# Decode pages in two rings, keys and values apart, with one rounding buffer fewer and the gates' cache laid out heads first

## The chip, the cores and the metric

The kernel runs on one core of one Trainium2 chip. The metric is the time of one execution on the device in microseconds (us); what is compared is the median of several executions. A trace of one execution, taken by the hardware profiler, gives the times of single instructions.

## The reference: what is computed

One step of a hybrid decoder layer, in 32-bit floating point, for two groups of rows that share the weights: a prompt of 1024 tokens, and eight samples with one new token each. Every row is normed and multiplied by `w_in`; the columns are the queries, keys, values and forget logits of 8 attention heads and the two inputs of 8 gating heads. The two groups of heads are normed, joined and multiplied by `w_o`. A cross attention with 4 heads into 256 memory tokens follows (`w_cq`, `w_co`), then a gated feed-forward network (ffn) with a causal convolution of width 3 (`w_up`, `w_down`, inner width 2816), and a final norm.

Each sample attends to its own past of 8192 tokens, which lies in 64 pages of 128 tokens:

```python
k_all = jnp.concatenate([k_pool[page_table].reshape(B, past, H, hd), k.astype(k_pool.dtype)], axis=1)
v_all = jnp.concatenate([v_pool[page_table].reshape(B, past, H, hd), v.astype(v_pool.dtype)], axis=1)
lf_all = jnp.concatenate([logf_pool[page_table].reshape(B, past, H).astype(jnp.float32), logf], axis=1)
c = jnp.cumsum(lf_all, axis=1)
```

The scores get the difference of the running sums `c` of the forget logits (the gates) before the softmax. Per sample that is 16 MB of keys and 16 MB of values, read once.

## The kernel before

The prompt and the samples are two streams of work. The prompt comes in stages: projections (`p1`), attention of two groups of rows, then for each half of 512 rows the output product of `w_o` (`mid`), the cross attention with its own output product (`out_proj` with `w_co`, L1063 to L1083), and the ffn. A large product on TensorE (PE) is made of three passes (L272 to L274, or L280, L281 and L284 where only half the rows are ready): a weight tile `wr` comes from memory (four buffers), ScalarE (ACT) rounds it into `wh` (L235, `WH` = 5 buffers), VectorE (DVE) makes the rest `wl` (L236, four buffers). Rows are normed and split in the same way: after the cross attention, DVE adds the product to the row (L1015), the row is scaled by its norm's factor (ACT, or DVE in L1045), PE turns it (L1124), and ACT and DVE split it (L238, L239) for the first products of `w_up`.

The samples' stream is `decode()`: for each sample 16 key steps and, a sample and two steps later (`VLAG`), 16 value steps in pairs. A key step (`kstep`) gathers a page of 1 MB (128 partitions x 2048 numbers) by an indirect DMA of GpSimd (POOL, L1428); DVE multiplies it by the query (L1444, in place) and sums over a head (L1448), in two pieces each in some stages. A value step (`vstep`) gathers its page (L1489), and PE multiplies it by the softmax's weights into one accumulator `dv` (L1495). All pages lie in one pool of `NKV` = 4 buffers, `kv`, and so do the weights and memory pages that the samples use later (L1568) and the prompt's rows at the start (L401). A page can be fetched when the one that had its buffer has been used. POOL issues the gathers in order; an issue whose buffer is not free holds up the ones behind it.

The gates of a sample are loaded at its 12th key step (L1404), brought from the order (token, head) into (head, token) by a copy on ACT (L1407), and scanned on DVE (L1408). They, the query tiles, the masks of `dv` and small tiles of the later stage share a pool of five 512-wide buffers, `d2`. The softmax of a sample is eight small steps on DVE (from L1460 on) with ACT and PE between.

The two streams are woven together by a table of paces: after so many units of the prompt's work, one step of the samples' stream is written. The framework then sets each engine's order with a model of times of its own, so buffers and priorities, not the code's order alone, decide what stands where. When the last sample is done, `sample_rest` takes the samples through `w_o`, the cross attention, and the ffn beside the prompt's second ffn.

## Time and profile before

| what | value |
| --- | --- |
| runs shown | 1798.83, 1797.29, 1791.11 us; median 1797.29 |
| profiled execution | 1793.69 us, span of its instructions 1791.7 us |
| mean granted clock of TensorE | 0.993 |
| moved by DMA | 521.06 MB, 291 GB/s in the mean |
| POOL's queue of gathers and pages | 341.14 MB, 50.0% of the DMA engines' time |
| SP's queue of weights | 165.73 MB, 26.5% |

PE is the engine with the most work. Its instructions run in the order written, and one that waits holds up all behind it; the same is true of the other engines. An idle gap in front of an instruction is put down to what released it, so the reader can ask at each gap whose work came last. The prediction uses three kinds of answers of the trace: the busy time of each engine in stretches of the span, the waits (engine, line, what it waited for, total, times, longest), and single instructions in order of time (start, duration, engine, line).

### The profile page before, as it was taken

To read this page: it belongs to the slowest core of one execution; us is meant where nothing else is said; L and a number is where in the kernel's file an instruction comes from. 1 tells how busy PE (TensorE), PEld (TensorE's weight loads), DVE (VectorE), ACT (ScalarE), POOL (GpSimd) and SP (SyncE) were. 2 spreads that over 40 slices of the span, in tenths; PEclk is the share of its full clock that TensorE was granted. 3 is DMA by queue.
4 is the path that set the end of the run, shared out by engine and by line. 5 is a ranking of instruction groups with operands and counts; after the bars stand their busy time and mean duration, and the time that the engine had idled before them with its cause. 6 is when DMAs were issued, how large, how long until landed. Compare 5 with 4: busy or idle time off the path is not lost.

```text
span 1791.7 us, 25124 instructions
## 1 busy us (share of the span) xinstructions
PE 1735.9 (97%) x9653; PEld 1285.7 (72%) x9653; DVE 1399.9 (78%) x1733; ACT 733.5 (41%) x1374; POOL 488.3 (27%) x461
## 2 busy tenths in 40 slices
PE   8999999889999999999999999999999999999997
PEld 5787777655677666767777777766666778768875
DVE  4689658989788986989999999898885549855344
ACT  6332355566643635333333244335353233333232
POOL 1252234443222332333322223433322112102110
PEclk9999999999999999999999999999999999999999
DMA  8786798777697975779788788988879587568982
GB/s 291 297 304 226 294 334 319 259 264 244 254 403 279 363 299 224 282 285 345 290 301 313 291 317 311 376 306 346 320 280 350 214 306 249 191 260 297 359 310 80
DMA packets 157074, 521.06 MB, mean 291 GB/s; under 512 B 20874, under 2 KB 40842, under 8 KB 124186
## 3 DMA queue, kind: packets, MB, share of 16 engines
q0 software_dynamic: 57168, 341.14, 50.0%
q1 hardware_dynamic: 92874, 165.73, 26.5%
q10 hardware_dynamic: 6912, 12.59, 1.9%
q8 instruction: 76, 1.25, 0.3%
q14 instruction: 44, 0.36, 0.1%
HBM read 495.47 MB, written 23.93 MB: 290 GB/s over the span
## 4 chain that ended last, share of the span: by engine, by line
PE 53%; issue 9%; DMA 8%; DVE 6%; ACT 2%; POOL 2%; POOLq 0%; DVEq 0%; ACTq 0%; SPq 0%
DMA kv<-cache_v,io 6%; PE ba L272 6%; PE ba L274 6%; PE ba L273 6%; PE dv L1495 4%; PE bb L272 3%; PE bb L273 3%; PE bb L274 3%; PE ba L1063 1%; DVE s L1448 1%; PE ba L1064 1%; PE ba L1065 1%; PE dv L331 1%; DMA kv<-cache_k,io 1%; PE dv L1774 1%
## 5 line engine op out<-in xcount | busy, mean ns | idle before, releaser
L235 ACT ACTIVATE wh<-wr 128x1024 fp32r<-128x1024 f32 (+2 forms) x220 | 228.6, 1044 | 443.3 <-PE ba L273 142.3
L236 DVE TENSOR_TENSOR wl<-wr,wh 128x1024 fp32r<-128x1024 f32 (+2 forms) x220 | 262.7, 1200 | 165.1 <-PE ba L274 57.4
L1428 POOL DMA_INDIRECT kv<-cache_k,io x128 | 186.9, 1460 | 606.8 <-DVE s L1448 327.2
L1444 DVE TENSOR_TENSOR kv<-kv,d 128x1024 f32<-128x1024 f32 (+1 forms) x156 | 258.0, 1681 | 32.6 <-DMA kv<-cache_k,io 32.6
L1448 DVE TENSOR_REDUCE s<-kv 128x16 f32<-128x1024 f32 (+1 forms) x156 | 258.4, 1672 | 0.0
L1489 POOL DMA_INDIRECT kv<-cache_v,io x128 | 160.8, 1256 | 239.4 <-PE dv L1495 155.2
L272 PE MATMUL ba<-u,wh 128*128 128x512 f32 x528 | 209.3, 397 | 0.0
L274 PE MATMUL ba<-u,wl 128*128 128x512 f32 x528 | 209.0, 396 | 0.0
L273 PE MATMUL ba<-u,wh 128*128 128x512 f32 x528 | 208.5, 395 | 0.5 <-DVE u L239 0.5
L272 PE MATMUL ba<-wh,u 128*128 128x512 f32 (+1 forms) x495 | 186.1, 379 | 0.9 <-ACT u L235 0.9
L273 PE MATMUL ba<-wl,u 128*128 128x512 f32 (+1 forms) x495 | 185.1, 375 | 1.3 <-DVE wl L236 1.3
L274 PE MATMUL ba<-wh,u 128*128 128x512 f32 (+1 forms) x495 | 183.4, 375 | 0.0
L1495 PE MATMUL dv<-kv,s 128*32 128x512 f32 x1024 | 127.1, 598 | 1.6 <-DMA kv<-cache_v,io 1.6
L274 PEld LDWEIGHTS ba<-u,wl 128*128 128x128 f32 x528 | 99.2, 188 | 29.0 <-issue 6.5
L272 PEld LDWEIGHTS ba<-u,wh 128*128 128x128 f32 x528 | 99.3, 188 | 26.4 <-issue 4.8
L273 PEld LDWEIGHTS ba<-u,wh 128*128 128x128 f32 x528 | 99.2, 188 | 25.2 <-issue 2.3
L272 PEld LDWEIGHTS ba<-wh,u 128*128 128x128 f32 x495 | 93.0, 188 | 25.0 <-issue 6.5
L272 PE MATMUL bb<-u,wh 128*128 128x512 f32 x272 | 108.7, 400 | 0.0
L274 PE MATMUL bb<-u,wl 128*128 128x512 f32 x272 | 108.0, 398 | 0.0
L273 PE MATMUL bb<-u,wh 128*128 128x512 f32 x272 | 107.9, 397 | 0.0
L273 PEld LDWEIGHTS ba<-wl,u 128*128 128x128 f32 x495 | 93.0, 188 | 20.1 <-DVE wl L236 1.9
L274 PEld LDWEIGHTS ba<-wh,u 128*128 128x128 f32 x495 | 92.9, 188 | 19.5 <-issue 1.6
(454 smaller groups left out, 3310.6 us busy)
## 6 DMA issues: line engine op xcount, KB each, us to landing
wr<-w_up SPq DMA_DIRECT2D x88, 512.0 KB
kv<-w_up POOLq DMA_DIRECT2D x22, 1024.0 KB
wr<-w_down SPq DMA_DIRECT2D x40, 512.0 KB
kv<-w_down POOLq DMA_DIRECT2D x11, 1024.0 KB
wr<-w_in SPq DMA_DIRECT2D x16, 512.0 KB
wr<-w_o SPq DMA_DIRECT2D x16, 512.0 KB
wr<-w_cq SPq DMA_DIRECT2D x16, 512.0 KB
wr<-w_co SPq DMA_DIRECT2D x16, 512.0 KB
```

The source lines that it names most:

```text
L235: nc.scalar.activation(h, src, AF.Copy)
L236: nc.vector.tensor_tensor(l, src, h.bitcast(F32), op=ALU.subtract)
L272: mmul(out, sh, mh, start=(i == 0), stop=False)
L273: mmul(out, sh, ml, start=False, stop=False)
L274: mmul(out, sl, mh, start=False, stop=(i == n - 1))
L331: mmul(ps[32 * j : 32 * j + 32, :w], xT[:, k, :] if nk == 8 else xT[:, k * 8 : k * 8 + 32], raw[:, q, j * w : (j + 1) * w], start=(k == 0) ...
L1063: mmul(pss[i], mh[k][:, tb], wh, start=(k == korder[0]), stop=False)
L1428: nc.gpsimd.indirect_dma_start(kv, None, a["cache_k"], off(kidx[:, b, ch : ch + 1]))
L1444: nc.vector.tensor_tensor(kvv[:, i : i + m, :], kvv[:, i : i + m, :], qb.unsqueeze(1).broadcast_to((P, m, 512)), op=ALU.mult)
L1448: nc.vector.tensor_reduce(s[:, ch * 4 + i : ch * 4 + i + m, :].rearrange("p k h -> p (k h)"), kvv[:, i : i + m, :].rearrange("p k (h d) -> ...
L1489: nc.gpsimd.indirect_dma_start(kv, None, a["cache_v"], off(kidx[:, b, ch : ch + 1]))
L1495: mmul(dv[32 * j : 32 * j + 32, :], s[:, ch * 4 : ch * 4 + 4, :].rearrange("p k h -> p (k h)"), kvv[:, j, :], start=(ch == 1), stop=(ch == ...
```

## The change

The page buffers become two rings, `kk` with two buffers for keys and `kv` with three for values; whatever else took a page buffer now takes from the two rings in turn, two of five from `kk`. That is one buffer of 8192 bytes a partition more; `wh` goes from five to four buffers (4160 bytes) and `d2` from five to three (4096 bytes). The gates' cache is laid out heads first before the launch, so the load at the ninth key step writes the tile that is scanned at the 12th, and the copy on ACT is gone. The two pages of a pair of values are no longer swapped in every second pair, and the accumulation's last matmul is marked accordingly. In the changed kernel all lines of these parts stand ten or nine later: L1428 is L1437, L1444 is L1453, L1448 is L1457, L1489 is L1498, L1495 is L1504, L235 is L245, L236 is L246, L239 is L249, L1015 is L1025, L1045 is L1055, L1404 is L1414.

```diff
--- before.py
+++ after.py
@@ -48,11 +48,12 @@
 
 
 
-NKV = 4
+NKK = 2
+NKV = 3
 VLAG = 2
 MIXR = 1.0
 G0R = 0.0
-WH = 5
+WH = 4
 WL = 4
 WR = 4
 TV = (0.0, 0.25)
@@ -120,8 +121,17 @@
     def T2(n=512, dt=F32):
         return tpool.tile([P, 512], dt, tag="t2", bufs=NT, name=nm("t2"))[:, :n]
 
+    def KK():
+        return dpool.tile([P, 2048], F32, tag="kk", bufs=NKK, name=nm("kk"))
+
+    def VV():
+        return dpool.tile([P, 2048], F32, tag="kv", bufs=NKV, name=nm("kv"))
+
+    ring = [0]
+
     def KV():
-        return dpool.tile([P, 2048], F32, tag="kv", bufs=NKV, name=nm("kv"))
+        ring[0] += 1
+        return KK() if ring[0] % 5 in (2, 4) else VV()
 
     def sm(shape, tag, bufs=2, dt=F32):
         return small.tile(shape, dt, tag=tag, bufs=bufs, name=nm(tag))
@@ -156,7 +166,7 @@
         return psum.tile([P, 512], F32, tag="dv", bufs=1, name=nm("dv"))
 
     def D2(n=512, dt=F32):
-        return dpool.tile([P, 512], dt, tag="d2", bufs=5, name=nm("d2"))[:, :n]
+        return dpool.tile([P, 512], dt, tag="d2", bufs=3, name=nm("d2"))[:, :n]
 
     def pair(tag):
 
@@ -1399,14 +1409,13 @@
             s = dpool.tile([P, 512], F32, tag="s", bufs=3, name=nm("s")).rearrange("p (k h) -> p k h", h=8)
             return qb, s
 
-        def gates_scan(b):
-            lg = D2()
-            nc.gpsimd.indirect_dma_start(lg, None, a["cache_logf"], off(lidx[:, b : b + 1]))
+        def gates_load(b):
             A = D2()
-            Ah = A.rearrange("p (h k) -> p h k", k=64)
-            nc.scalar.activation(Ah, lg.rearrange("p (k h) -> p h k", h=8), AF.Copy)
+            nc.gpsimd.indirect_dma_start(A, None, a["cache_logf"], off(lidx[:, b : b + 1]))
+            return A
+
+        def gates_scan(A):
             nc.vector.tensor_tensor_scan(A, rmask, A, 0.0, op0=ALU.mult, op1=ALU.add)
-            return A
 
         def gates(b, A):
             tot = sm([P, 8], "tot", 2)
@@ -1424,7 +1433,7 @@
 
         def kstep(b, ch, st):
             qb, s = st
-            kv = KV()
+            kv = KK()
             nc.gpsimd.indirect_dma_start(kv, None, a["cache_k"], off(kidx[:, b, ch : ch + 1]))
             kvv = kv.rearrange("p (k c) -> p k c", c=512)
             if phase[0][:3] == "att":
@@ -1497,7 +1506,7 @@
                             s[:, ch * 4 : ch * 4 + 4, :].rearrange("p k h -> p (k h)"),
                             kvv[:, j, :],
                             start=(ch == 1),
-                            stop=(ch == 15),
+                            stop=(ch == 14),
                             tile_position=(0, 32 * j),
                         )
 
@@ -1535,8 +1544,10 @@
             left = 1
             if b < 8:
                 left = yield from kstep(b, ch, st[b])
+                if ch == 8:
+                    A[b] = gates_load(b)
                 if ch == 11:
-                    A[b] = gates_scan(b)
+                    gates_scan(A[b])
                 if ch == 13:
                     dt_[b] = gates(b, A[b])
                 if ch == 14 and b < 7:
@@ -1553,9 +1564,7 @@
             if 0 <= vb < 8 and vch % 2:
                 if vch == 1:
                     dv[vb] = DV()
-                two = [(vch - 1, KV()), (vch, KV())]
-                if vch % 4 == 3:
-                    two.reverse()
+                two = [(vch - 1, VV()), (vch, VV())]
                 pend += [vstep(vb, c, st[vb], dv[vb], kv) for c, kv in two]
             yield left
 
@@ -1987,7 +1996,7 @@
     return {
         "x": f(x), "xT": f(x.T), "xs": f(xs), "xsT": f(xs.T.reshape(8, P, 8).transpose(1, 0, 2)),
         "cache_k": f(n["cache_k"]).reshape(-1, 4 * AW), "cache_v": f(n["cache_v"]).reshape(-1, 4 * AW),
-        "cache_logf": f(n["cache_logf"]).reshape(-1, 64 * NH),
+        "cache_logf": f(n["cache_logf"].reshape(-1, 64, NH).transpose(0, 2, 1)).reshape(-1, 64 * NH),
         "cmk": f(n["cache_mem_k"][0]).reshape(NB, NMEM, D), "cmv": f(n["cache_mem_v"][0]).reshape(NB, NMEM, D),
         "stT": f(n["state_conv"][0].transpose(2, 1, 0).reshape(2 * NF, P, 16).transpose(1, 0, 2)),
         "pt": f(n["page_table"].T), "mem": f(n["mem_prompt"][0]), "memT": f(n["mem_prompt"][0].T),
```

The change moves instructions on POOL, DVE and ACT; three places follow, of before and of the change. The first is the start of POOL's row: `r1r` is the norm factor of the samples' rows, `rstd` those of the prompt's, `kv` and `kk` the page buffers. Before:

```order
L223 TENSOR_TENSOR r1r_237<-r1r_237,mhalf 8x1
L1428 DMA kv_348<-cache_k,io 128x2048
L1428 DMA kv_388<-cache_k,io 128x2048
L412 TENSOR_TENSOR rstd_123<-xv_252,mhalf 128x4
L412 TENSOR_TENSOR rstd<-xv_255,mhalf 128x4
L1428 DMA kv_453<-cache_k,io 128x2048
L1428 DMA kv_485<-cache_k,io 128x2048
L412 TENSOR_TENSOR rstd_123<-xv_266,mhalf 128x4
L412 TENSOR_TENSOR rstd<-xv_269,mhalf 128x4
L1404 DMA d_132_1075<-cache_logf,lidx 128x512
L1404 DMA d_390_2464<-cache_logf,lidx 128x512
```

With the change:

```order
L233 TENSOR_TENSOR r1r_237<-r1r_237,mhalf 8x1
L1498 DMA kv_1595<-cache_v,io 128x2048
L1437 DMA kk_348<-cache_k,io 128x2048
L1498 DMA kv_1596<-cache_v,io 128x2048
L422 TENSOR_TENSOR rstd_123<-xv_252,mhalf 128x4
L422 TENSOR_TENSOR rstd<-xv_255,mhalf 128x4
L1437 DMA kk_388<-cache_k,io 128x2048
L1498 DMA kv_1699<-cache_v,io 128x2048
L422 TENSOR_TENSOR rstd_123<-xv_266,mhalf 128x4
L422 TENSOR_TENSOR rstd<-xv_269,mhalf 128x4
L1414 DMA d_117_843<-cache_logf,lidx 128x512
L1437 DMA kk_453<-cache_k,io 128x2048
```

Three value pages are now issued among the first key pages, one of them ahead of the first key page, and the first load of gates stands ahead of the third key page.

The second place is DVE at the end of the second half's cross attention, where its rows are normed and split for the ffn; `d` is the query, `s` the scores, `wl` the rests of weights, `u` the prompt's rows. Before:

```order
L1444 TENSOR_TENSOR kv_10825<-kv_10825,d_1841_9748 128x1024 x2
L236 TENSOR_TENSOR wl_11031<-wr_11029,wh_11032 128x1024
L1448 TENSOR_REDUCE s_9750<-kv_10825 128x16 x2
L236 TENSOR_TENSOR wl_11217<-wr_11215,wh_11218 128x1024
L236 TENSOR_TENSOR wl_11276<-wr_11274,wh_11277 128x1024
L1460 TENSOR_TENSOR s_9750<-s_9750,dec_10745 128x512
L1462 TENSOR_REDUCE pm_10832<-s_9750 128x8
L239 SCALAR_TENSOR_TENSOR u_11037<-ba_11038,gp,u_11036 128x256
L239 SCALAR_TENSOR_TENSOR u_11048<-bb_11049,gp,u_11047 128x256
L239 SCALAR_TENSOR_TENSOR u_11059<-ba_11060,gp,u_11058 128x256
L239 SCALAR_TENSOR_TENSOR u_11037<-ba_11038,gp,u_11036 128x256
L239 SCALAR_TENSOR_TENSOR u_11070<-ba_11071,gp,u_11069 128x256
```

With the change:

```order
L249 SCALAR_TENSOR_TENSOR u_11043<-ba_11044,gp,u_11042 128x256
L1453 TENSOR_TENSOR kk_10719<-kk_10719,d_1834_9734 128x1024 x2
L246 TENSOR_TENSOR wl_11317<-wr_11315,wh_11318 128x1024
L249 SCALAR_TENSOR_TENSOR u_11054<-ba_11055,gp,u_11053 128x256
L249 SCALAR_TENSOR_TENSOR u_11021<-ba_11022,gp,u_11020 128x256
L249 SCALAR_TENSOR_TENSOR u_11032<-bb_11033,gp,u_11031 128x256
L1457 TENSOR_REDUCE s_9736<-kk_10719 128x16
L249 SCALAR_TENSOR_TENSOR u_11043<-ba_11044,gp,u_11042 128x256
L1453 TENSOR_TENSOR kk_10771<-kk_10771,d_1834_9734 128x1024 x2
L1055 TENSOR_SCALAR u_11089<-u_9507,fac_2067_11010 128x512 x2
L1457 TENSOR_REDUCE s_9736<-kk_10719 128x16
L249 SCALAR_TENSOR_TENSOR u_11054<-ba_11055,gp,u_11053 128x256
```

Before, the last key step (L1444, L1448) and the softmax's first two steps (L1460, L1462) stood ahead of the first split (L239). Now the splits begin first, two key steps lie among them and the scaling of the last row (L1055), and the last key step stands further on, ahead of the last two splits:

```order
L249 SCALAR_TENSOR_TENSOR u_11032<-ba_11111,gp,u_11031 128x256
L249 SCALAR_TENSOR_TENSOR u_11043<-ba_11120,gp,u_11042 128x256
L249 SCALAR_TENSOR_TENSOR u_11054<-bb_11129,gp,u_11053 128x256
L1453 TENSOR_TENSOR kk_10809<-kk_10809,d_1834_9734 128x1024 x2
L249 SCALAR_TENSOR_TENSOR u_11021<-bb_11094,gp,u_11020 128x256
L1457 TENSOR_REDUCE s_9736<-kk_10809 128x16 x2
L249 SCALAR_TENSOR_TENSOR u_11021<-bb_11094,gp,u_11020 128x256
L1469 TENSOR_TENSOR s_9736<-s_9736,dec_10729 128x512
L1471 TENSOR_REDUCE pm_10816<-s_9736 128x8
```

The third place is POOL where keys end and only values are left; `fac` are the norm factors of the prompt's rows there, `w_o` are weight pages of the samples' next product. Before, from the end of the values on:

```order
L1489 DMA kv_11381<-cache_v,io 128x2048
L1489 DMA kv_11380<-cache_v,io 128x2048
L1489 DMA kv_11433<-cache_v,io 128x2048
L1489 DMA kv_11434<-cache_v,io 128x2048
L1489 DMA kv_11483<-cache_v,io 128x2048
L1489 DMA kv_11482<-cache_v,io 128x2048
L1568 DMA kv_11670<-w_o 128x2x1024
L1568 DMA kv_11672<-w_o 128x2x1024
L1568 DMA kv_11727<-w_o 128x2x1024
L1568 DMA kv_11729<-w_o 128x2x1024
```

With the change, around the last keys:

```order
L1498 DMA kv_10969<-cache_v,io 128x2048
L1498 DMA kv_11187<-cache_v,io 128x2048
L1042 TENSOR_TENSOR fac_2062_10996<-fac_2062_10996,mhalf 128x1
L1437 DMA kk_10719<-cache_k,io 128x2048
L1437 DMA kk_10771<-cache_k,io 128x2048
L1042 TENSOR_TENSOR fac_2066_11007<-fac_2066_11007,mhalf 128x1
L1042 TENSOR_TENSOR fac_2067_11010<-fac_2067_11010,mhalf 128x1
L1437 DMA kk_10809<-cache_k,io 128x2048
L1577 DMA kk_11656<-w_o 128x2x1024
L1577 DMA kk_11713<-w_o 128x2x1024
L1498 DMA kv_11188<-cache_v,io 128x2048
L1498 DMA kv_11236<-cache_v,io 128x2048
```

The weight pages that fall to the key ring are now issued right behind the last key page, ahead of the last fifteen value pages; those in the value ring still come behind them, and a key page stands behind value pages less often.

## The prediction

> **What bounds the kernel now.** I read the page's busy shares and chain first, then the busy time by stages, and then the waits, TensorE's ahead of the others'.
>
> ```profile
> PE 1735.9 (97%) x9653; PEld 1285.7 (72%) x9653; DVE 1399.9 (78%) x1733; ACT 733.5 (41%) x1374; POOL 488.3 (27%) x461
> PE 53%; issue 9%; DMA 8%; DVE 6%; ACT 2%; POOL 2%; POOLq 0%; DVEq 0%; ACTq 0%; SPq 0%
> ```
>
> TensorE (PE) is busy for 1735.9 of 1791.7 us, and 53% of the chain that ended last is its own work. The change takes no matmul from it, so a gain can come only out of the 55.8 us in which PE stands idle, and a loss only where PE is made to wait more. Where that idle time lies is read from the busy time by stages (window, its length, then PE, PEld, DVE, ACT and POOL, PE's clock, and the DMA engines' share and GB/s):
>
> ```profile
> 0.00:15.00 15.00, 7.85 (x29) 4.61 (x29) 7.73 (x28) 8.76 (x12) 0.98 (x6) 1.00 0.72 230
> 15.00:30.00 15.00, 15.00 (x67) 10.13 (x64) 8.65 (x19) 7.55 (x11) 0.00 (x0) 1.00 0.71 240
> 30.00:60.00 30.00, 29.57 (x143) 22.84 (x142) 4.92 (x10) 14.93 (x26) 10.15 (x10) 1.00 0.99 397
> 1100.00:1350.00 250.00, 241.43 (x1236) 172.46 (x1224) 216.86 (x256) 111.51 (x232) 86.62 (x66) 1.00 0.86 328
> 1320.00:1330.00 10.00, 8.62 (x61) 5.83 (x59) 9.96 (x17) 6.17 (x14) 4.15 (x4) 1.00 0.97 392
> 1330.00:1340.00 10.00, 8.65 (x57) 7.37 (x58) 6.43 (x17) 5.95 (x15) 0.55 (x1) 1.00 0.50 206
> 1350.00:1480.00 130.00, 130.00 (x720) 90.75 (x720) 65.61 (x102) 41.48 (x68) 23.80 (x31) 1.00 0.77 288
> 1480.00:1550.00 70.00, 69.08 (x301) 55.87 (x300) 69.14 (x86) 25.66 (x43) 11.72 (x19) 1.00 0.71 241
> ```
>
> The start, 0 to 15 us, has 7.15 us of the idle time. The second half's output products and cross attention (1100 to 1350) have 8.57, of which 2.73 lie in only 20 us, 1320 to 1340, where VectorE (DVE) is busy for 9.96 of the first 10. From 1350 to 1480 PE has no gap at all. So the places that can move the time are the start, 1100 to 1350 and the narrow 1320 to 1340. The waits for pages stand beside that:
>
> ```profile
> POOL kv L1428 <- DVE s L1448: 327.2, 68, 28.2
> POOL kv L1489 <- PE dv L1495: 155.2, 41, 11.4
> POOL kv L1428 <- PE dv L1495: 127.5, 18, 14.7
> DVE kv L1444 <- DMA kv<-cache_k,io: 32.6, 18, 5.6
> DVE kv L1444 <- DMA kv<-cache_k,io: 15.8, 9, 3.7
> PE dv L1495 <- DMA kv<-cache_v,io: 1.6, 2, 1.3
> PEld dv L1495 <- DMA kv<-cache_v,io: 2.3, 2, 1.7
> ```
>
> Each row gives the engine and line, what it waited for, microseconds in total, times, longest. POOL's waits for a free buffer are long but hurt nobody by themselves: POOL is busy for 27% of the span. What they delay is the page. DVE loses 32.6 us to key pages not yet there, 15.8 of it from 1100 to 1350 (the second such row, from that window alone), and PE itself loses only 1.6 + 2.3 = 3.9 us to value pages.
>
> **The change part by part.** *Two rings.* In before, a key page sometimes waits for a value page's matmul: 127.5 us over 18 times. That goes, and with it, at best, PE's 3.9 us for value pages, since three buffers are now theirs; at worst nothing of it. I take -2. For keys, two buffers must be enough. The rows of 1100 to 1350 price that:
>
> ```profile
> 1151.20 2.81 POOL L1428 DMA_INDIRECT kv<-cache_k,io  x1 [8.50 <-DVE s L1448]
> 1296.79 0.94 POOL L1428 DMA_INDIRECT kv<-cache_k,io  x1 [1.59 <-DVE s L1448]
> 1094.06 11.44 DMA kv<-cache_k,io
> 1237.66 9.73 DMA kv<-cache_k,io
> 1315.04 2.36 DVE L1444 TENSOR_TENSOR kv<-kv,d 128x1024 f32<-128x1024 f32 x2 [1.01 <-DMA kv<-cache_k,io]
> 1318.46 2.34 DVE L1448 TENSOR_REDUCE s<-kv 128x16 f32<-128x1024 f32 x2
> ```
>
> The first two are the first and the last of 19 key issues in a row, (1296.79 - 1151.20) / 18 = 8.1 us apart, so a ring of two has 16.2 us for a page's whole round. A round is the page's way from issue to landing (9.73 and 11.44 us in the two rows from the chain) and the multiply and reduce, 2.36 + 2.34 = 4.7 us: 14.4 to 16.1 us. That just fits. The ring of two is on its limit, and not clearly beyond it.
>
> [...]
>
> What the rings do to order is seen in the rows ahead of this prediction. Around 1285 to 1300 us the new order has done 3 to 4.5 key steps fewer on DVE than before at the same rounding of a weight. The last key step of all stood ahead of the softmax and ahead of the splits of the cross output's norm (L239); now three key steps stand among those splits, and the last split comes behind them.
>
> ```profile
> 1324.72 0.47 DVE L239 SCALAR_TENSOR_TENSOR u<-ba,gp,u 128x256 fp32r<-128x256 f32 x1
> 1326.43 0.39 PE L280 MATMUL ba<-u,wh 128*128 128x256 f32 x1 [1.05 <-DVE u L239]
> 1322.98 0.68 DVE L1460 TENSOR_TENSOR s<-s,dec 128x512 f32<-128x512 f32 x1
> 1333.75 1.08 DVE L1485 TENSOR_REDUCE lps<-s 128x8 f32<-128x512 f32 x1
> 1337.50 0.46 DVE L239 SCALAR_TENSOR_TENSOR u<-bb,gp,u 128x256 fp32r<-128x256 f32 x1
> ```
>
> PE follows those splits closely: its first matmul of the ffn (L280) started 1.7 us after the first split and had waited 1.05 us for it. From 1320 to 1340 DVE is busy for 9.96 + 6.43 = 16.4 us. Three key steps add 3 x 4.7 = 14.1. The last sample's softmax leaves the stretch: eight small pieces, of which the two rows are the first and the last, 4.3 us together. So 26.2 us of work would stand where 20 were: 6 us late. The ends: nothing, if DVE enters the stretch early by as much because it did fewer keys ahead of it; 12, if each of the three pages also lets DVE wait, as the 1.01 us in the row above and 5.6 at the longest show. DVE was only about a microsecond behind PE on entry, so I take **+6**. On the other side, the fewer keys from 1150 to 1300 relieve DVE where PE idled 8.57 - 2.73 = 5.8 us. I take -2 of it (0 to -5.8).
>
> *The first value page.* At the start POOL's row now has a value page ahead of the first key page, and nothing but its index holds it (the first row is the last work on the index).
>
> ```profile
> 15.59 0.68 DVE L1390 CUSTOM_DVE_ANT_0 io<-l,io 128x32 uint16<-128x32 uint16 x7
> 36.35 1.17 POOL L1428 DMA_INDIRECT kv<-cache_k,io  x1 [22.49 <-DMA kv<-x]
> 29.81 2.74 DVE L239 SCALAR_TENSOR_TENSOR u<-wr,gp,u 128x512 fp32r<-128x512 f32 x4 [3.65 <-ACT u L238]
> 35.18 0.40 PE L272 MATMUL ba<-wh,u 128*128 128x512 f32 x1
> ```
>
> So 1 MB is issued near 15.59 + 0.68 = 16.3 us, not after 36.35. At 397 GB/s (30 to 60 us) it is 2.6 us of the DMA engines, ahead of weights and prompt rows. The prompt's second half is split by 29.81 + 2.74 = 32.55 and first used at 35.18, so 2.6 us of slack cover it; from 15 to 30 us the DMA engines are also free for 29%. 0 to +2.6; I take +1.
>
> *One rounding buffer fewer.* ACT may round a weight tile only when the tile four back, not five, has been used.
>
> ```profile
> L235 ACT ACTIVATE wh<-wr 128x1024 fp32r<-128x1024 f32 (+2 forms) x220 | 228.6, 1044 | 443.3 <-PE ba L273 142.3
> 547.99 1.06 ACT L235 ACTIVATE wh<-wr 128x1024 fp32r<-128x1024 f32 x1
> 564.46 1.06 ACT L235 ACTIVATE wh<-wr 128x1024 fp32r<-128x1024 f32 x1 [1.70 <-PE bb L273]
> ```
>
> ACT has 443.3 us of idle time ahead of these roundings and mostly waits for PE, so it is ahead by nearly a whole buffer. Going through all tiles (when each was rounded, when the buffer four back was let go, when it was first used), one is caught clearly: the tile rounded at 547.99, whose buffer would be free only when the next row's was, about 564, while PE uses it from 562. That is some 2 to 3.5 us if PE's order has nothing between. Far end: one rounding of 1.04 us lost at each of several changes of product, about +5. I take +1.5.
>
> *The gates' copy.* It was eight copies on ACT and their wait for the load:
>
> ```profile
> ACT d L1407 <- DMA d<-cache_logf,lidx: 18.1, 3, 8.8
> L1407 ACT ACTIVATE d<-d x8: 1116/1214/1265, 68.7 to 1228.5; 128x512 f32<-128x512 f32 x8
> DVE d L1408 <- ACT d L1407: 4.7, 4, 1.7
> ```
>
> ACT loses 8 x 1.2 + 18.1 = 28 us of work and waits. ACT is at 41%, and no wait of PE's own names this line, so I take 0 of it; the most would be the 4.7 us that DVE waited. The load now comes three key steps ahead of its scan, 24 us, which covers it. *The smaller pool of 512-wide tiles* (five to three) has one tile fewer to hold, the copy's source; a query tile or a mask that waits for a buffer waits on SP or DVE under a 16-step cycle. 0.
>
> *The tail.* When the keys are done, the values have three buffers where they had four. Pairs were issued at these times, and at three more between:
>
> ```profile
> 1357.00 0.94 POOL L1489 DMA_INDIRECT kv<-cache_v,io  x1 [3.20 <-PE dv L1495]
> 1388.54 0.94 POOL L1489 DMA_INDIRECT kv<-cache_v,io  x1 [5.70 <-PE dv L1495]
> ```
>
> That is (1388.54 - 1357.00) / 4 = 7.9 us a pair; with three buffers of four, 10.5. Some eight pairs give 8 x 2.6 = 21 us later for the last one. PE's order already puts each pair later behind prompt products, and PE has no gap there. I take 0, with +13 at the far end, if PE comes to a pair and its page isn't there.
>
> **Sum.** The profiled execution took 1793.69 us (span 1791.7 and 2.0 around it). -2 + 6 - 2 + 1 + 1.5 + 0 + 0 = +4.5. The medians' three runs and this one have a mean of 1795.2, 2.1 under the median; on that mean the sum is **1800**, 0.15% above the median, which half a per cent (9 us, about what a measurement of this kernel can tell from no change) doesn't separate.
>
> **The rivals.** *Faster: the rings free the keys.* DVE's 32.6 us of waits for key pages shrink because a key page no longer queues behind a value page's buffer (the 127.5 us), the three steps in the norm are absorbed by an earlier DVE, and PE's 8.57 us of 1100 to 1350 go: 1795.2 - 8.6 = 1787. For it speaks that row of 18 waits; against it, that the round of 14.4 to 16.1 us leaves two key buffers next to nothing to win in that stage. Chance 0.2.
>
> *Nothing: the change doesn't do what it says.* The four buffers already served as two and two, since a pair of values holds two of them from issue to matmul; the order on PE stays and every term above is covered: 1795. For it speaks the row of 155.2 us: a pair of values already waits for little but the pair ahead of it. Chance 0.14, beside 0.36 for my forecast.
>
> *Slower: a ring of two is too short.* It decides when a page takes over 16.2 - 4.7 = 11.5 us from issue to landing. At 13 to 14 us a round is 1.5 to 2.5 over; the 19 issues counted above are 9.5 rounds, so the keys fall 14 to 24 us behind, DVE stands at a key multiply with splits queued behind it, and PE, which idled 8.57 us where DVE waited 15.8 for pages, would idle for about half of it: +7 to +12, 1807 to 1812. For it speaks 11.44 us in the chain; against it, that at most three value pages now share the DMA engines with a key. Chance 0.2.
>
> *Slower: the tail.* The +13 of the value pairs on PE in order, with DVE at 69.14 of 70 us right behind (1480 to 1550) so that nothing is caught up: 1800 + 13 = 1813, or less. Chance 0.1.
>
> **How the numbers follow.** Likeliest is the forecast, 1800. The cases hold 0.2 under 1788 (faster by over 0.5%), 0.3 over 1806 from the two slow rivals and a little of the forecast's own far end, 0.03, and the rest, 0.47, between. The range reaches from 1785 to 1814, from the fast rival with 2 us for its bounds to the slow ones.
>
> **What would show it.** In the profile after: the idle time of PE from 1320 to 1340 and the rows of L249 and L1453 in it (right if PE's gap there grows by 4 to 8 us); DVE's wait for kk pages at L1453 (32.6 before; over 60 means the short ring); PE's wait for value pages at L1504 (3.9 before; over 10 means the tail); the start of the product that used the second half at 35.18; PE's waits for L245 near 560. The forecast is wrong if PE's idle time in total stays at 55.8 us or falls, or if it grows by over 12 us elsewhere than there.

## The result, and the profile after

The change makes the kernel slower: 1841.91 us median of five runs (1837.77 to 1846.79) against 1797.29 before, a ratio of 1.0269 with an interval of 1.0236 to 1.0301. The profiled execution took 1841.91 us, 48.2 more than that of before. The page of after, busy time and chain:

```profile
PE 1758.6 (96%) x9653; PEld 1295.4 (70%) x9653; DVE 1397.8 (76%) x1733; ACT 727.7 (40%) x1370; POOL 492.5 (27%) x461
PE 68%; DMA 11%; DVE 9%; issue 6%; ACT 3%; POOL 1%; SPq 1%; ACTq 0%; POOLq 0%; DVEq 0%
```

TensorE ran the same 9653 matmuls, and yet its busy time grew by 22.7 us, while its idle time grew from 55.8 to 1840.1 - 1758.6 = 81.5, by 25.7. The two together are the loss, and nearly half of it is no waiting at all. The mean granted clock says what the first half is: 0.993 before, 0.981 now, and (1 - 0.981) x 1840.1 - (1 - 0.993) x 1791.7 = 22.4 us. Stages of after (window, length, then PE, PEld, DVE, ACT, POOL, PE's clock, DMA share, GB/s):

```profile
30.00:60.00 30.00, 29.45 (x136) 22.95 (x135) 3.91 (x9) 15.12 (x26) 8.96 (x9) 1.00 1.03 413
110.00:130.00 20.00, 14.87 (x76) 10.55 (x74) 14.97 (x13) 8.41 (x11) 3.21 (x3) 0.83 0.70 259
1350.00:1360.00 10.00, 6.53 (x37) 4.86 (x36) 9.68 (x13) 7.53 (x18) 2.96 (x3) 1.00 0.99 386
1360.00:1370.00 10.00, 6.81 (x34) 5.74 (x34) 10.00 (x15) 2.37 (x6) 1.75 (x2) 0.66 0.37 107
1370.00:1380.00 10.00, 5.84 (x26) 4.84 (x26) 8.40 (x12) 1.46 (x4) 0.74 (x2) 0.83 0.47 176
1380.00:1500.00 120.00, 120.00 (x633) 83.89 (x635) 62.28 (x94) 43.72 (x64) 18.01 (x18) 1.00 0.66 234
```

The start is as it was, and from 1380 to 1500 us PE has no gap, though the last values go through three buffers there. Between, PE idles in narrow places and is slow around them. From 1350 to 1380, the norm that the prediction named, it idles for 10.8 us, and the clock falls to 0.66. From 110 to 130 us it idles for 5.1, where before had no gap to speak of:

```profile
110.00:130.00 20.00, 19.92 (x99) 14.41 (x98) 18.23 (x15) 8.29 (x11) 12.41 (x5) 1.00 0.94 312
```

That place is the clearest. POOL's issues, DVE's key step and PE's wait behind it, in after:

```profile
106.17 2.75 POOL L1437 DMA_INDIRECT kk<-cache_k,io  x1 [7.26 <-DVE s L1457]
115.46 2.29 DVE L1453 TENSOR_TENSOR kk<-kk,d 128x2048 f32<-128x2048 f32 x1 [5.03 <-DMA kk<-cache_k,io]
120.13 2.35 DVE L246 TENSOR_TENSOR wl<-wr,wh 128x1024 fp32r<-128x1024 f32 x2
121.40 0.80 PE L283 MATMUL bb<-wl,u 128*128 128x512 f32 x1 [5.13 <-DVE wl L246]
121.99 0.63 PE L284 MATMUL bb<-wh,u 128*128 128x512 f32 x1
126.89 0.39 PE L284 MATMUL bb<-wh,u 128*128 128x512 f32 x1
```

The page is issued when a key buffer comes free, lands 9.3 us later, DVE stands 5.03 us at the multiply, the rest of a weight (L246) is queued behind the key step, and PE stands 5.13 us for it. Then the same matmul takes 0.63 us where a little later it takes 0.39: from 121.4 to 126.6 us the granted clock is 0.50. The three value pages issued early lie in their buffers all that time; the first is used at 208 us. Four keys were fetched at a time here before, and two are now:

```profile
79.05 0.95 POOL L1428 DMA_INDIRECT kv<-cache_k,io  x1 [28.18 <-DVE s L1448]
81.24 0.95 POOL L1428 DMA_INDIRECT kv<-cache_k,io  x1 [1.25 <-DVE s L1448]
83.44 0.94 POOL L1428 DMA_INDIRECT kv<-cache_k,io  x1 [1.25 <-DVE s L1448]
85.63 1.88 POOL L1428 DMA_INDIRECT kv<-cache_k,io  x1 [1.25 <-DVE fl L513]
78.70 0.94 POOL L1437 DMA_INDIRECT kk<-cache_k,io  x1 [26.49 <-DVE s L1457]
80.89 0.94 POOL L1437 DMA_INDIRECT kk<-cache_k,io  x1 [1.25 <-DVE fl L523]
```

The first four rows are of before, the last two of after. Counting each page from its issue to its last use, the pool of before held four keys up to about 160 us, then about two keys and two values up to 1300, and up to four values at the end; after holds about two keys and three values from 50 us to the end of the keys. From 60 to 130 us DVE never waited for a key page in before, and does so for 8.6 us now.

The same shape comes back in the first half's cross attention, where ACT waits for a piece of DVE's (L1200) that stands behind the key step, and PE for ACT:

```profile
649.59 2.36 DVE L1453 TENSOR_TENSOR kk<-kk,d 128x1024 f32<-128x1024 f32 x2 [5.35 <-DMA kk<-cache_k,io]
652.59 0.48 ACT L1203 ACTIVATE cbs<-cmx,rq 128x1 f32<-128x1 f32 x2 [6.75 <-DVE cmx L1200]
658.71 1.22 PE L1226 MATMUL ba<-u,t 128*128 128x512 f32 x1 [3.55 <-ACT u L1219]
```

And in the second half's norm three key steps stand among the splits, ahead of the split (L249) that PE waits for. The first waits 0.32 us for its page and the third 1.27; the second and the third are shown:

```profile
1362.02 2.35 DVE L1453 TENSOR_TENSOR kk<-kk,d 128x1024 f32<-128x1024 f32 x2
1372.55 2.36 DVE L1453 TENSOR_TENSOR kk<-kk,d 128x1024 f32<-128x1024 f32 x2 [1.27 <-DMA kk<-cache_k,io]
1374.83 0.48 DVE L249 SCALAR_TENSOR_TENSOR u<-bb,gp,u 128x256 fp32r<-128x256 f32 x1
1375.36 0.51 PE L283 MATMUL ba<-u,wh 128*128 128x512 f32 x1 [3.14 <-DVE u L249]
```

Waits for pages in after, in total:

```profile
POOL kk L1437 <- DVE s L1457: 426.5, 82, 26.5
POOL kv L1498 <- PE dv L1504: 311.5, 55, 16.4
DVE kk L1453 <- DMA kk<-cache_k,io: 50.8, 24, 5.4
PE dv L1504 <- DMA kv<-cache_v,io: 0.9, 1, 0.9
PEld dv L1504 <- DMA kv<-cache_v,io: 2.1, 2, 1.8
```

DVE waits 50.8 us for key pages (32.6 before); PE waits 3.0 us for value pages (3.9 before). Compared matmul by matmul (the same one in both traces, at its time in before), after is 2 us late at 108 us, 9.6 at 133, 12 at 283, 19 at 434, 20.5 at 536, 28.5 at 561, 32 at 636, 31 from there to 1320, 40 at 1345 and 47 at 1623. The loss is made in some seven or eight narrow places, and the long products between them add nothing.

### The profile page after: what moved, and what is told of

Same layout as the page of the kernel before. It is cut to its first block, busy times and chain, and to the rows that moved or that the text cites. A ratio compares the mean times of both kernels' runs of the same rounds, so it can differ in the third digit from the quotient of the medians.

```text
span 1840.1 us, 25073 instructions
## 1 busy us (share of the span) xinstructions
PE 1758.6 (96%) x9653; PEld 1295.4 (70%) x9653; DVE 1397.8 (76%) x1733; ACT 727.7 (40%) x1370; POOL 492.5 (27%) x461
## 4 chain that ended last, share of the span: by engine, by line
PE 68%; DMA 11%; DVE 9%; issue 6%; ACT 3%; POOL 1%; SPq 1%; ACTq 0%; POOLq 0%; DVEq 0%
PE ba L283 9%; PE ba L282 9%; PE ba L284 9%; DMA kk<-cache_k,io 7%; PE dv L1504 5%; PE bb L282 5%; PE bb L283 5%; PE bb L284 5%; DVE kk L1453 2%; DVE wl L246 1%; PE dv L341 1%; DVE s L1457 1%; PE ba L1073 1%; PE dv L1783 1%; PE ba L1074 1%
## 5 line engine op out<-in xcount | busy, mean ns | idle before, releaser
L245 ACT ACTIVATE wh<-wr 128x1024 fp32r<-128x1024 f32 (+2 forms) x220 | 228.5, 1044 | 467.5 <-PE ba L283 151.8
L246 DVE TENSOR_TENSOR wl<-wr,wh 128x1024 fp32r<-128x1024 f32 (+2 forms) x220 | 262.2, 1200 | 160.6 <-ACT wh L245 160.3
L1437 POOL DMA_INDIRECT kk<-cache_k,io x128 | 185.1, 1446 | 568.2 <-DVE s L1457 426.5
L1453 DVE TENSOR_TENSOR kk<-kk,d 128x1024 f32<-128x1024 f32 (+1 forms) x156 | 258.6, 1682 | 51.0 <-DMA kk<-cache_k,io 50.8
L1498 POOL DMA_INDIRECT kv<-cache_v,io x128 | 169.4, 1323 | 344.1 <-PE dv L1504 311.5
L1457 DVE TENSOR_REDUCE s<-kk 128x16 f32<-128x1024 f32 (+1 forms) x156 | 258.8, 1673 | 0.3
L282 PE MATMUL ba<-wh,u 128*128 128x512 f32 (+1 forms) x495 | 188.4, 382 | 1.9 <-ACT u L245 0.9
L284 PE MATMUL ba<-wh,u 128*128 128x512 f32 (+1 forms) x495 | 185.3, 379 | 1.8 <-DVE u L246 1.8
L1504 PE MATMUL dv<-kv,s 128*32 128x512 f32 x1024 | 128.6, 604 | 1.6 <-DMA kv<-cache_v,io 0.9
L282 PEld LDWEIGHTS ba<-wh,u 128*128 128x128 f32 x495 | 94.4, 191 | 25.7 <-issue 4.2
L283 PEld LDWEIGHTS ba<-wl,u 128*128 128x128 f32 x495 | 94.2, 190 | 22.8 <-issue 4.6
```

Source lines behind the costliest of these rows:

```text
L245: nc.scalar.activation(h, src, AF.Copy)
L246: nc.vector.tensor_tensor(l, src, h.bitcast(F32), op=ALU.subtract)
L282: mmul(out, sh, mh, start=(i == 0), stop=False)
L283: mmul(out, sh, ml, start=False, stop=False)
L284: mmul(out, sl, mh, start=False, stop=(i == n - 1))
L1437: nc.gpsimd.indirect_dma_start(kv, None, a["cache_k"], off(kidx[:, b, ch : ch + 1]))
```

## The experiments

Theory A: two key buffers are too few. Theory B: four rounding buffers are too few. Theory C: any edit makes the framework choose another, worse order; theory D, its opposite, that a part costs what the buffers it takes away are worth. Ratios are to before, on the same chip. The diffs show the lines that matter.

**The parts alone.** Each of these is the kernel before with one edit. Two rings of two buffers:

```diff
-NKV = 4
+NKK = 2
+NKV = 2
-            kv = KV()
+            kv = KK()
-                two = [(vch - 1, KV()), (vch, KV())]
+                two = [(vch - 1, VV()), (vch, VV())]
```

> The kernel before with its four page buffers parted into two for keys and two for values, nothing else changed (five rounding buffers, five 512-wide tiles, the copy of the gates, the swapped pairs). Theory A: as slow as the change or slower, 1830 to 1855 us, with VectorE's wait for key pages at 45 us or more. Theory B: 1797, no change. Theory C: 1805 to 1840, by chance.

Measured 1.0273 (1.0250 to 1.0296), 1842.04 us: parting the same four buffers alone costs as much as the whole change. That is theory A's size, with 44.0 us of waits for key pages, but not all of it is the keys': 16 of the 54 us of lateness arise from 1575 to 1610 us, when the last key step (1356 us) is long done. And two key buffers don't make the gap at 121 us by themselves: PE is busy for all of 110 to 130 us here, and DVE waits 1.9 us for a key page from 60 to 130.

Four rounding buffers:

```diff
-WH = 5
+WH = 4
```

> The kernel before with four rounding buffers in place of five, nothing else. Theory A: 1795 to 1803 us, a few microseconds at most near 560 us. Theory B: 1820 or more. Theory C: 1805 to 1840 by chance.

Measured 1.0152 (1.0119 to 1.0185), 1822.49 us: about 27 us, where theory A and the prediction had a few. Theory A is not all. One of its gaps is a rounding's own: the tile's buffer comes free only when the product ahead ends, so its rest (L236) falls among the splits of a norm. Another is a value page that comes late:

```profile
1197.30 0.39 PE L281 MATMUL bb<-u,wl 128*128 128x256 f32 x1 [3.42 <-DVE wl L236]
591.07 1.08 PE L1495 MATMUL dv<-kv,s 128*32 128x512 f32 x4 [3.31 <-DMA kv<-cache_v,io]
```

Three 512-wide tiles:

```diff
-        return dpool.tile([P, 512], dt, tag="d2", bufs=5, name=nm("d2"))[:, :n]
+        return dpool.tile([P, 512], dt, tag="d2", bufs=3, name=nm("d2"))[:, :n]
```

> The kernel before with three 512-wide tiles in place of five; nothing else. The order of TensorE stays the same up to the end of the keys and differs after. Theory D (the smaller pool costs nothing, as predicted, or costs at the samples' cross attention near 1480 to 1550): 1790 to 1800 us. Theory C: 1795 to 1815, the loss behind 1300 us alone.

Measured 1.0077 (1.0049 to 1.0106), 1806.71 us. Both theories were wrong on the place: the first gap lies at 166 us. Two queries, the gates' load and its copy want four tiles, and with three the load is late, ACT stands at the copy, and PE behind it:

```profile
160.18 1.19 ACT L1407 ACTIVATE d<-d 128x512 f32<-128x512 f32 x1 [9.00 <-DMA d<-cache_logf,lidx]
165.99 0.79 PE L272 MATMUL ba<-wh,u 128*128 128x512 f32 x1 [3.50 <-ACT t L469]
```

In the change the copy is gone, and with it the fourth tile; there POOL's issues of this load wait 0.8 us for a tile, once. So this cost belongs to the part alone.

The gates' layout, and the pairs no longer swapped:

```diff
-            nc.scalar.activation(Ah, lg.rearrange("p (k h) -> p h k", h=8), AF.Copy)
```

```diff
-                if vch % 4 == 3:
-                    two.reverse()
-                            stop=(ch == 15),
+                            stop=(ch == 14),
```

> The kernel before with the gates' cache laid out heads first and its load put three key steps ahead of the scan, the copy on ScalarE gone; buffers as before. It takes work away. Theory D: 1785 to 1795 us, a little faster or equal. Theory C: 1800 to 1830, since the order changes from the first gates' load on.

> The kernel before with the pairs of value pages no longer swapped in every second pair; nothing else. Theory D: 1790 to 1797 us. Theory C: little too, since the order of TensorE changes only inside the pairs (some 400 of 7056 rows): 1788 to 1805.

Measured 1.0028 (1.0010 to 1.0045) and 1.0003 (0.9982 to 1.0025). Taking eight copies and their waits from ACT won nothing; it came out a few microseconds slower than theory D said.

**Is it any order?** One pace of the table, with no buffer touched:

```diff
-PACE = {'p1': 7.0, 'att0': 12.0, 'attx': 26.0, 'mid0': 8.0, 'ffn0': 8.5, 'att1': 11.0, 'mid1': 6.8, 'ffn1': 2.5, 'rest': 2.9}
+PACE = {'p1': 7.0, 'att0': 12.0, 'attx': 26.0, 'mid0': 8.1, 'ffn0': 8.5, 'att1': 11.0, 'mid1': 6.8, 'ffn1': 2.5, 'rest': 2.9}
```

> The kernel before with one number of the table of paces changed from 8.0 to 8.1 (the first half's output product and cross attention); no buffer, no instruction and no byte changes, only the order in which the two streams are woven from 500 us on. Theory C (the order before is a good one among many, and any edit that makes the framework choose again loses): 1800 to 1830 us, with new idle gaps of TensorE behind VectorE or ScalarE after 500 us. Theory D (the losses belong to the buffers taken away): within 5 us of before, 1788 to 1798.

Measured 1.0015 (1.0000 to 1.0030). At least 1705 of TensorE's 9653 matmuls stand at another place in the trace (compared by line, tile names and shape), a gap of 4.80 us appears at 1265 us, and yet only some 3 us came of it; the gates' layout, with a gap of 4.44 us at 1263, cost 5. So theory C is unlikely as the main cause; two orders are few, and as a part of a loss it isn't excluded. Two more runs take the buffer away and hold one engine to before's order, by an order edge between neighbours:

```diff
+    for rows in ROW.values():
+        for x, y in zip(rows, rows[1:]):
+            tc.add_manual_dep(
+                ins[y], ins[x].name, mybir.DependencyInfo(mybir.DependencyClass.NoSync, mybir.DependencyReason.DATA), reason="row"
+            )
```

> The kernel before with four rounding buffers, as in e4_wh4, but VectorE's instructions held in exactly the order they have in before; the other engines' orders are chosen again. If the loss of four rounding buffers (1.5%) comes from another order on VectorE: 1793 to 1802 us. If it comes from the missing buffer, or from what TensorE and ScalarE must then do in another order: 1815 to 1830 again.

> The kernel before with two rings of two buffers, as in e3_rings22, but TensorE's instructions held in exactly the order of before; the other engines' orders are chosen again. If the loss of the rings (2.7%) is the missing buffers (a key page must wait where it waited for nothing): 1835 to 1860 us, since TensorE can't even step aside. If it is the order chosen for TensorE: 1795 to 1810.

Measured 1.0192 (1.0175 to 1.0209) and 1.0318 (1.0296 to 1.0339): with the order of before held on that engine, each is no better than with the order chosen for it. That speaks for the missing buffer itself, or for the orders of the other engines, which no run held. In f3_pe the tail shows as well, with two buffers for values and PE not free to step aside:

```profile
PE dv L1507 <- DMA kv<-cache_v,io: 23.9, 10, 4.9
```

**The change, taken back in pieces.** One pool of five, one pool of four (the rest of the change kept):

```diff
-        return dpool.tile([P, 2048], F32, tag="kk", bufs=NKK, name=nm("kk"))
+        return dpool.tile([P, 2048], F32, tag="kv", bufs=NKV, name=nm("kv"))
-NKV = 3
+NKV = 5
```

```diff
+NKV = 4
```

> The change with its two rings made one again: one pool of five page buffers for keys and values; four rounding buffers, three 512-wide tiles and the gates' layout stay as in the change. Theory A (two key buffers are too few: VectorE stands at a key multiply, TensorE goes idle behind it and its clock is halved for some microseconds after): the loss goes, 1785 to 1800 us, VectorE's wait for key pages at the multiply under 35 us (50.8 in the change), no idle gap of TensorE over 3 us near 115 us. Theory B (four rounding buffers are the loss): stays near 1835 to 1842. Theory C (any new pool sizes upset the order that the framework's model of times picks): still 15 to 45 us over before, with the gaps in other places.

> The change without rings and without the fifth page buffer: one pool of four pages, four rounding buffers, three 512-wide tiles, the new layout of the gates. If the losses are those of the parts taken away (rounding buffer alone 1.5%, smaller tile pool 0.8%, gates 0.3%): 1830 to 1840 us, and the fifth buffer bought nearly nothing, since the pool of five took 1832. If the fifth buffer bought what it should: 1840 to 1855. If the parts overlap rather than add: 1815 to 1825.

Measured 1.0216 (1.0189 to 1.0243) with five and 1.0130 (1.0106 to 1.0154) with four. DVE's wait for key pages was 22.8 us with five, as theory A had it, and the kernel was slow all the same, so theory A alone falls here; and the fifth buffer, for which the others were given, made a shared pool slower. With four, the parts overlap, as the third case had it. Why five are slower is open: its largest gaps (5.7 us at 576, 4.2 at 500, 4.1 at 1128) lie behind splits and a load of gating rows, not behind pages.

The ends. The first sample's keys from both rings, in the change:

```diff
-            kv = KK()
+            kv = KV() if b == 0 else KK()
```

> The change, with the first sample's 16 key pages taken from both rings in turn (as the weight pages are), so that they have five buffers as long as no value is due. Theory A: the 7.5 us of lateness that arise near 115 to 125 us go, and what arises later stays: 1828 to 1836 us; the first PE gap over 3 us then lies after 300 us. Theory B: no change from 1842. Theory C: any time from 1815 to 1850, with the gaps after 300 us in other places.

Measured 1.0213 (1.0185 to 1.0241), 1831.08 us, as theory A had it: the place at 121 us is gone.

```profile
110.00:130.00 20.00, 18.99 (x97) 13.51 (x96) 20.00 (x15) 10.01 (x13) 14.01 (x4) 1.00 0.94 327
```

Three buffers for keys and two for values, and then both ways with both ends open (the last sample's values from both rings too):

```diff
-NKK = 2
-NKV = 3
+NKK = 3
+NKV = 2
```

```diff
-                two = [(vch - 1, VV()), (vch, VV())]
+                two = [(c, KV() if vb == 7 else VV()) for c in (vch - 1, vch)]
```

> The change with its five page buffers parted the other way, three for keys and two for values. Theory A (two key buffers are too few): faster than the change, 1825 to 1835 us, VectorE's wait for key pages under 35 us (50.8), no gap of TensorE over 3 us near 121 us. Rival (values suffer more than keys gain): 1840 to 1860, with TensorE's own wait for value pages over 10 us (1.6 in the change).

> The change with three buffers for keys and two for values, and with both rings open to the first sample's keys and the last sample's values. If the rings lose at the ends (e6_first won 0.6% at the start; e5_rings32 was level with before until 1700 us and lost 40 us at the end, in waits for the samples' last weights): 1792 to 1812 us. If the middle loses: 1825 to 1840, no better than e5_rings32.

> The change itself (two buffers for keys, three for values) with both rings open to the first sample's keys and the last sample's values. If two key buffers are too few in the middle: 1825 to 1835, like e6_first, with the waits near 650 and 1280 us left. If the loss is at the ends: 1800 to 1815.

Measured: e5_rings32 1.0226 (1.0197 to 1.0255), e17_32ends 1.0127 (1.0107 to 1.0146), e18_23ends 1.0199 (1.0174 to 1.0224). DVE's wait for pages of the key ring in e5_rings32, in e17_32ends and in e18_23ends:

```profile
DVE kk L1453 <- DMA kk<-cache_k,io: 5.5, 4, 3.0
```

```profile
DVE kk L1453 <- DMA kk<-cache_k,io: 4.7, 3, 2.4
```

```profile
DVE kk L1453 <- DMA kk<-cache_k,io: 37.5, 18, 4.9
```

With three key buffers the wait is nearly gone. e5_rings32 then loses at the other end: with two buffers in the tail the samples' stream ends late, and when the prompt is done PE still waits for the samples' last weights. From 1780 us to its end PE is idle for 28.7 us there, against 10.4 in e17_32ends. Until then it had been late too (11 us at 700, 24 at 1275); its prompt draws level with before near 1650 because the samples' products then stand behind it. Some of the waits at the end:

```profile
PE dv L341 <- DMA kk<-w_down: 6.3, 4, 2.2
```

With both ends open that goes, and 1.0127 is left, what the shared pool of four has with the same rounding buffers (1.0130). With two key buffers and open ends it is 1.0199, and the gaps in the middle stay, 3.6 us at 642 and 11.4 in the norm. So two key buffers in place of three cost 0.7% in the middle, and closed ends another 0.7% (1.0269 - 1.0199), nearly all of it the start (1.0269 - 1.0213 in e6_first). Most of the middle's 0.7% is the norm: in e17_32ends PE idles for 0.5 us from 1320 to 1380 us, and no lateness arises there. Before, too, had about two buffers for keys in the middle; why a fixed two costs more than a shared two is not shown.

**The clock by itself.** Behind the end of before, 18 blocks of matmuls, each waiting for a chain of ScalarE copies of the one ahead:

```diff
+    for k in (0, 1, 2, 3, 4, 6) * 3:
+        ps = BK()
+        for i in range(44):
+            mmul(ps, t[:, :P], t, start=(i == 0), stop=(i == 43))
+        t = U([P, 512], F32R)
+        nc.scalar.activation(t, ps, AF.Copy)
+        for i in range(k):
+            nc.scalar.activation(t, t.bitcast(F32), AF.Copy)
```

> The kernel before, and behind its end 18 blocks of 44 equal 512-column matmuls on TensorE, each of which waits for a chain of ScalarE copies of the block ahead of it, so that TensorE idles for about 1 to 5 us between blocks, each length three times; the outputs stay as they are, and only the 200 us at the end are read. If idle time itself halves the clock: gaps under about 1.5 us are followed by full speed, gaps over 2.5 us by some microseconds at half speed, losing about 1.7 us or twice that each, as after the gaps of the change. If the low stretches come from heat or power and not from gaps: the low stretches stand in the blocks at random, or not at all.

Each row is one block: its start, its duration, and in brackets the idle time ahead of it.

```profile
1804.36 10.27 PE L1954 MATMUL ba<-u 128*128 128x512 f32 x44 [0.69 <-ACT u L1956]
1815.97 10.27 PE L1954 MATMUL bb<-u 128*128 128x512 f32 x44 [1.35 <-ACT u L1958]
1828.24 10.27 PE L1954 MATMUL ba<-u 128*128 128x512 f32 x44 [2.01 <-ACT u L1958]
1841.19 11.62 PE L1954 MATMUL ba<-u 128*128 128x512 f32 x44 [2.67 <-ACT u L1958]
...
1907.55 11.88 PE L1954 MATMUL ba<-u 128*128 128x512 f32 x44 [2.01 <-ACT u L1958]
...
1954.93 12.71 PE L1954 MATMUL ba<-u 128*128 128x512 f32 x44 [4.65 <-ACT u L1958]
...
2005.16 13.18 PE L1954 MATMUL ba<-u 128*128 128x512 f32 x44 [2.67 <-ACT u L1958]
```

After 0.69 and 1.35 us the block took 10.27 us, all six times. After 2.01 it was longer once in three times, after 2.67 always, after 3.33 twice in three, after 4.65 both times, by 1.35 to 2.91 us (one execution). So the idle time itself does it here; 2.01 us is the shortest gap of these blocks that did.

The gap's length alone doesn't decide it. In the traces of before, after, f3_pe, f4_dve, e17_32ends and e18_23ends the low stretches, at a clock of 0.50, begin whole multiples of 3.41 us apart and, ahead of the end, last one to three times 3.41 us. Of the three gaps of 2.01 us, the one ahead of 1907.55, with the longer block behind it, lay in one step of this raster (1905.5 to 1908.9); the other two lay across two steps. And no long gap was needed. In after there are twelve low stretches ahead of the end; in the 3.41 us ahead of each PE was busy for 53% or less, and six of them have no single gap over 1.83 us in the two steps ahead. One of the six, the step ahead and the step itself:

```profile
1283.73:1287.14 3.41, 1.61 (x8) 0.61 (x7) 3.41 (x6) 2.15 (x7) 0.72 (x1) 1.00 1.00 411
1287.14:1290.55 3.41, 3.41 (x19) 0.87 (x18) 3.41 (x4) 3.41 (x13) 0.79 (x2) 0.50 0.89 314
```

The border is not sharp: in before and after, of 1023 steps at full clock behind the first 15 us, those in which PE was busy for less than 45% were always followed by a low one, and those with over 54% never; in e17_32ends one with some 58% (63.4 to 66.8 us) was.

## Why the prediction was wrong

It named two of the mechanisms and their places, one in the forecast and one as a rival, and was too low on three terms. Its own sign of being wrong came: PE's idle time grew by 25.7 us, of which 8.1 lie in the norm and so 17.6, over its 12, elsewhere.

- **The three key steps in the norm, +6.** Right in place and cause. PE idles 10.8 us from 1350 to 1380, against 2.73 from 1320 to 1340 before: +8.1. With the clock, some 10 us of lateness arise there. The bound was 12. The prediction priced it beside the short ring, but it is the ring that puts the key steps there: with three key buffers (e17_32ends) the last softmax (L1469) starts at 1314.95, ahead of DVE's first split of that norm (1336.74), and with two (e18_23ends) three key steps stand among the splits again.
- **DVE relieved ahead of the norm, -2; the tail, 0.** In the stretch ahead of the norm (1100 to 1320 before, 1131 to 1351 after) PE idles 2.55 us in place of 5.84, as forecast, but after is 31 us late at both ends of it. In the tail the pairs are issued 10.9 us apart, as forecast (10.5), and PE has no gap.
- **One rounding buffer fewer, +1.5.** This step failed. Alone it costs 27 us (1.0152), and with the smaller tile pool and the gates' layout 23 (1.0130). The prediction asked of each tile whether its rounding would still be ready at its first use, and found one of 220 caught. It took the order for given. But the new order is not free: in a norm, tiles are in use across two products, and what five buffers let ACT and DVE do ahead of the norm now falls into it (3.42 us at 1197 in e4_wh4). How the other gaps of that run follow from the buffer, among them 9.2 us of value pages, is not shown.
- **Two rings, -2, and the rival of the short ring.** This step failed as much: alone, two rings of two cost 49 us (1.0273). The value pages' 3.9 us fell only to 0.9 + 2.1 = 3.0. The round of 14.4 to 16.1 us in 16.2 was the wrong test. It priced the steady stage alone, where four shared buffers were already about two and two. Where only keys are under way the old pool gave them all four, and where only values are, again all four; the prediction saw this for the tail and not for the start, where it counted the early value page's bytes (+1; no lateness over 2 us came of them until 108 us) and not the three buffers that the value pages then hold. Closed ends cost 0.7%, the middle another 0.7% (13 us). A ring of two is too short, as the rival had it, but that its +7 to +12 came near these 13 us is luck: it wanted pages that take 13 to 14 us in the stage ahead of the norm, where from 1131 to 1350 they take 9.1 in the median and no lateness arises; and its sign, over 60 us of waits for key pages, didn't come (50.8).
- **The price of an idle microsecond.** All terms were sums of waits, with nothing for the clock. Of the 48 us, 22.7 are PE's longer busy time, which its slower clock accounts for (22.4). The rows at 121 us show both: 5.13 us of wait, and 5 us of matmuls at 0.63 in place of 0.39. A step of 3.41 us at a clock of 0.50 that PE works through costs half of its length, 1.7 us, as an estimate from these two numbers; in e16_clock the blocks took 1.35 to 2.91 us longer. PE need not have been idle for a whole step: ahead of the low one at 1287.14 in after it was busy for 1.61 of 3.41 us, and in e16_clock gaps of 2.01 and 2.67 us were enough. The prediction had quoted the clock's column and put nothing on it.
- **The gates' copy and the smaller pool, 0 each.** 0.3% and 0.8% as parts alone; the second is the copy's own tile, so that in the change it isn't there.

Taken away in one order, the parts make 1.3% (the rounding buffer with its companions, e2_shared4 and e17_32ends), 0.7% (two key buffers in place of three in the middle) and 0.7% (closed ends). The sum is the measured 2.7% because each share is the difference of two runs in a row. Alone, the parts cost 2.7, 1.5, 0.8 and 0.3%, twice the loss: they overlap, and in another order the shares would be others. No run gives the change its fifth rounding buffer back. The fifth page buffer gave nothing back. No version tried beats the kernel before.

## What to carry to other kernels

A shared pool serves each stream with all its buffers when the other has nothing under way; before parting it, look at the stages where one stream runs alone, and not at the steady one. When a buffer is taken from a helper that runs ahead (a rounding, a load), ask what it did ahead of the next narrow place, and not whether it would still be ready in the order of before. On this TensorE, 97% busy, 25.7 us more of idle time came with 22.4 us of slower clock, and in the blocks of e16_clock a gap of 2.01 us cost up to 1.61 us more and one of 2.67 up to 2.91. So price such a wait, or several short ones that leave TensorE less than about half busy for 3.41 us (1.61 us of it at 1283.73 in after), at up to about twice its length.

## What the runs showed of the hardware that was not expected

Behind an idle gap of TensorE of 2.01 us a block of matmuls took 11.88 us in place of 10.27, once in three times, and behind gaps of 0.69 and 1.35 us never (18 blocks of e16_clock, six of them behind such a short gap). The low stretches, at a clock of 0.50, begin whole multiples of 3.41 us apart, and six of the twelve in after came behind gaps of at most 1.83 us, with PE busy for 53% or less of the step ahead; the low clock costs 22 us more in after than in before. And another order on TensorE, with the buffers of before, moved the time by only 0.15 and 0.28% in p1_pace and e7_gates.
